# A two-layer hybrid decoder trunk: S5 block loads in a pool of their own, SSD's VectorE operations regrouped, the S5 scan on chunks between the MLA merges

## The chip, the cores and the metric

The kernel runs on one core of a Trainium2 chip. The metric is the device time of one execution in microseconds (us). Three executions of the kernel before took 1957.41 to 1961.91 us, median 1959.04.

## The reference

Each of the two layers normalises the 512 x 1024 input, multiplies it by one wide projection, and feeds three parallel causal branches: SSD (a chunked Mamba-2 scan), S5 (a diagonal complex recurrence) and MLA (latent attention). The branches are gated, summed, projected and added to the input.

```python
for l in range(2):
    h = rms_norm(x, pre_norm[l])
    z_a, xbc, dt_raw, u_b, z_b, c_q, c_kv, k_rope, z_c, gate_logits = split_columns(h @ w_in[l])
    y_a = ssd_branch(z_a, xbc, dt_raw, ...) @ w_a[l]
    y_b = s5_branch(u_b, z_b, ...) @ w_b[l]
    y_c = mla_branch(c_q, c_kv, k_rope, z_c, ...) @ w_c[l]
    g = sigmoid(gate_logits)
    x = x + rms_norm((g[0] * y_a + g[1] * y_b + g[2] * y_c) @ w_o[l], post_norm[l])
```

In SSD each head needs, for each chunk of 128 positions, exp(cs[t] - cs[s]) on and under the diagonal, multiplied with the product of C and B; x is scaled by dt, and by dt and the decay to the chunk's end for the chunk's state. In S5 the state of 64 blocks of 8 positions follows s[c+1] += a * s[c] with complex a.

## The kernel before, in words

Every float32 matrix product is made of three matmuls: each operand is split into a rounded part (`wh`, `hh`, `ah`, made by a ScalarE copy) and the rest (`wl`, `hl`, `al`, a VectorE subtraction). `split` (L83) does this for activations and `weight` (L92) for weights: a 512 KB load into a tile `wf`, the copy to `wh`, the subtraction to `wl`, each with two buffers. With `lo_pool` at n, GpSimd makes every n-th `wl` in place of VectorE, counted by `self.nw`. `dense` (L108) runs 24 matmuls of 512 columns on one weight: 16 on `wh`, then 8 on `wl`.

A layer goes through these stages: MLA, with the S5 preparation `s5_prep` filled in between; the S5 scan (`s5_scan`, L896) and the eight merges of MLA (`merge`, L470, on `w_c`, each with a gate tile); `ssd_dt` (L665), small operations for dt and its running sum; `ssd` (L723), four groups of four heads, in which the projections, the convolutions (`conv`, L739: one ScalarE and four VectorE operations on 512 columns), the heads (`head`, L848) and the states are dealt out in turn; the S5 stage (L1052), eight blocks of `silu2`, `s5_block` (L912), a merge on `w_a` and `s5_gelu`; then GLU, the merges on `w_b` and the output projection. In layer 0 the scan starts at 398 us, SSD fills about 450 to 683 us, the S5 stage 683 to 810 us; layer 1 comes some 967 us later.

All loads and stores go through SP's one queue, in order. Program order isn't the order of execution: the kernel is built under `TileContext(nc, schedule_with_timeline_sim=True)`, which lays out each engine's instructions in advance by a timeline of its own, with program order as the priority among those that are ready. Once laid out, every engine runs its instructions in that order and waits at each for what it needs.

The steps that matter here:
- The scan loads all states into `ms` (128 x 2 x 32 x 64, 2 MB), runs 63 steps of four VectorE operations on 64 elements each (L905 to L908), and stores to `sdr`. A step reads `ms[:, :, :, c]`: neighbouring elements lie 64 floats apart. In program order the scan comes ahead of the merges.
- `s5_block` loads for each block of eight groups `uf`, `sf` (from `sdr`), eight pieces of `kpad` and one of `odr`, 11 transfers and 1.5 MB, in the pool `s5`, which opens after the pool `ssd` has closed, and whose tiles take the same memory.
- `head` broadcasts one head's running sum by a matmul into `pr` (PSUM), subtracts the position's own sum and clamps at zero in four VectorE operations of 128 columns (L856), takes exp on ScalarE in one operation, multiplies and splits.
- `xe`, the state's input, is made by GpSimd from the product `xd` (L787).
- The SSD result `y` is multiplied by the norm's gain on VectorE (L844) and then split.

Of the kernel before, what the change touches and what calls it, by code (L numbers as in the profile page):

```python
# [9 lines left out]
F32 = mybir.dt.float32  # L10
F32R = mybir.dt.float32r
I32 = mybir.dt.int32
AF = mybir.ActivationFunctionType
ALU = mybir.AluOpType
# [6 lines left out]
P = 128  # L21
# [13 lines left out]
class Trunk:  # L35
# [629 lines left out]
    def ssd_dt(self, l, sp):  # L665

        nc, a, sm = self.nc, self.a, self.sm
        raw = sp.tile([P, 512], F32, name="dtraw")
# [46 lines left out]
        dte, dec = sp.tile([P, 64], F32, name="dte"), sp.tile([P, 64], F32, name="dec")  # L715
        self.tt(dte, ps[:, 0:64], cs, ALU.subtract)
        self.act_(dte, dte, AF.Exp)
        self.act_(dec, ps[:, 0:64], AF.Exp)
        self.tap(f"dt{l}", dt)
        self.tap(f"cs{l}", cs)  # L720
        return dt, cs, cs2, dte, dec

    def ssd(self, l):  # L723
        nc, tc, a = self.nc, self.tc, self.a
        with tc.tile_pool(name=f"ssd{l}", bufs=1, reuse_waits="tile") as sp:
            dt, cs, cs2, dte, dec = self.dts
            cw, cb = self.mgp.tile([P, 16, 4], F32, name="cw"), self.mgp.tile([P, 16], F32, name="cb")
            nc.sync.dma_start(cw, a["conv_w"][l])
            nc.sync.dma_start(cb, a["conv_b"][l])
# [27 lines left out]
            def core(g, xs, zs, bt, ct):  # L757
# [15 lines left out]
                for i in range(2):  # L773
                    ps = self.bank()
                    for c in range(4):
                        nc.tensor.transpose(ps[:, c * P:c * P + P], xs[i][:, c * P:c * P + P], self.ident)
                    xd = self.tmp().rearrange("p (c h d) -> p c h d", c=4, h=2)
                    hs = slice(4 * g + 2 * i, 4 * g + 2 * i + 2)
                    self.tt(
                        xd, ps.rearrange("p (c h d) -> p c h d", c=4, h=2),  # L780
                        cst(dt, 0, 4, hs).unsqueeze(3).broadcast_to([P, 4, 2, 64]), ALU.mult,
                    )
                    cc = slice(128 * i, 128 * i + 128)
                    xf = xd.rearrange("p c h d -> p c (h d)")
                    self.split(xf, xdh[:, :, cc], xdl[:, :, cc])
                    xe = sp.tile([P, 3, 2, 64], F32, name="xef", tag="xef")
                    self.gt(xe, xd[:, 0:3], cst(dte, 0, 3, hs).unsqueeze(3).broadcast_to([P, 3, 2, 64]), ALU.mult)  # L787
                    self.split(xe.rearrange("p c h d -> p c (h d)"), xeh[:, :, cc], xel[:, :, cc])
                    yield
                ps = self.bank()  # L790
# [20 lines left out]
                for i in range(2):  # L811
# [29 lines left out]
                    if pt:  # L841
                        self.gt(sq, sq, s2, ALU.add)
                    hi, lo = self.act_tile()
                    self.ts(y, y, sn[:, pt:pt + 1], None, ALU.mult)  # L844
                    self.split(y, hi, lo)
                    self.yacts.append((hi, lo))

            def head(g, hh, cbm):  # L848

                hd = 4 * g + hh  # L850
                pr = self.pq.tile([P, 512], F32, name="pr", tag=("pM", "pb")[hh % 2])
                nc.tensor.matmul(pr, self.sel[:, hd:hd + 1].broadcast_to([64, P]), cs2, start=True, stop=True)
                m = self.tmp()
                for c in range(4):
                    k = slice(c * P, c * P + P)
                    self.ts(m[:, k], pr[:, k], cs[:, 16 * c + hd:16 * c + hd + 1], 0.0, ALU.subtract, ALU.min)  # L856
                self.act_(m, m, AF.Exp)
                self.tt(m, m, cbm.rearrange("p c k -> p (c k)"), ALU.mult)
                mh, ml = r2("mm", [P, 512], 2)
                self.split(m, mh, ml)  # L860
                return mh, ml, pr
# [34 lines left out]
    def s5_scan(self, l, sp):  # L896

        nc = self.nc
        kpad, odr, msd, u2, sc1, sc2 = self.s5m[l]
        ms = sp.tile([P, 2, 32, 64], F32, name="ms")  # L900
        nc.sync.dma_start(ms, msd.rearrange("h p r g c -> (h p) r g c"))
        t1, t2 = sp.tile([P, 2, 32], F32, name="sc_t1"), sp.tile([P, 2, 32], F32, name="sc_t2")
        for c in range(63):
            s, d = ms[:, :, :, c], ms[:, :, :, c + 1]
            nc.vector.tensor_tensor(t1, sc1, s, ALU.mult)  # L905
            nc.vector.tensor_tensor(t2, sc2, s[:, ::-1], ALU.mult)
            nc.vector.tensor_tensor(d, d, t1, ALU.add)
            nc.vector.tensor_tensor(d, d, t2, ALU.add)  # L908
        self.sdr = self.dr.tile([2, 64, 2, 32, 64], F32, name=f"sdr{l}")
        nc.sync.dma_start(self.sdr.rearrange("h p r g c -> (h p) r g c"), ms)  # L910

    def s5_block(self, l, sp, b):  # L912

        nc, a = self.nc, self.a
        kpad, odr, msd, u2, sc1, sc2 = self.s5m[l]
        g8 = slice(8 * b, 8 * b + 8)

        def load(src, nm):
            f = sp.tile([P, 8, 64], F32, name=nm + "f", tag=nm + "f")
            nc.sync.dma_start(f, src)  # L920
            h, lo = (sp.tile([P, 8, 64], F32R, name=nm + x, tag=nm + x) for x in "hl")
            self.split(f, h, lo)
            return h, lo

        uh, ul = load(u2[b].rearrange("p (g c) -> p g c", g=8), "u")
        sh, sl = load(self.sdr[b // 4, :, :, 8 * (b % 4):8 * (b % 4) + 8].rearrange("p r g c -> r p g c"), "s")
        th, tl = self.weight([(slice(16 * j, 16 * j + 16), kpad[:, g8, 16 * j:16 * j + P]) for j in range(8)], 1024, sp)
        oh, ol = self.weight(odr[:, g8].rearrange("p g k -> p (g k)"), 1024, sp)
        ys = sp.tile([64, 8, 8, 16], F32, name="ys", tag="ys")
        pss = [self.pq.tile([P, 512], F32, name="pM", tag=tag) for tag in ("pM", "pb")]  # L930
        for hf in range(2):
# [78 lines left out]
    def mix(self, l):  # L1010
        nc, tc, a = self.nc, self.tc, self.a
        with ExitStack() as st:
# [27 lines left out]
                self.yacts.append((hi, lo))  # L1040
            acts, self.yacts = self.yacts, []
            with tc.tile_pool(name=f"scan{l}", bufs=1, reuse_waits="tile", side="right") as sp:
                self.s5_scan(l, sp)
                for m in range(8):
                    self.merge(l, 2, a["w_c"], acts, m)
            with tc.tile_pool(name=f"dt{l}", bufs=1, reuse_waits="tile") as dp:
                self.dts = self.ssd_dt(l, dp)
                self.lo_pool = 2
                self.ssd(l)
                self.lo_pool = 0  # L1050
            acts, self.yacts = self.yacts, []
            with tc.tile_pool(name=f"s5{l}", bufs=1, reuse_waits="tile") as sp:  # L1052
                G, gl = self.G, []
                for b in range(8):
                    if b < 6:
                        G.append(self.silu2(l, ZB + b + 2))
                    ys = self.s5_block(l, sp, b)
                    self.merge(l, 0, a["w_a"], acts, b, self.rrow)
                    gl.append(self.s5_gelu(l, sp, b, ys, G[b]))
                self.gates_ahead(l, 1, 2)  # L1060
                self.s5_glu(l, sp, gl, G)
            acts, self.yacts = self.yacts, []
            wp = st.enter_context(tc.tile_pool(name=f"wo{l}", bufs=1, reuse_waits="tile", side="right"))
            G = wp.tile([P, D], F32, name="gpost")
            nc.sync.dma_start(G, a["post_norm"][l:l + 1, :].broadcast_to([P, D]))
# [175 lines left out]
```

## Time and profile before

| | us |
|---|---|
| median of three executions | 1959.04 |
| lowest, highest | 1957.41, 1961.91 |
| the profiled execution | 1960.12 |
| its span, first to last instruction | 1958.3 |
| TensorE busy (matmuls) | 1855.4, 95% |
| VectorE busy | 1430.2, 73% |
| ScalarE busy | 913.1, 47% |
| GpSimd busy | 627.0, 32% |

[...] In what follows L12 is line 12 of the kernel, PE is TensorE, DVE VectorE, ACT ScalarE, POOL GpSimd, and SPq the queue from which SP issues transfers. Instructions are named by the tile that they write and those that they read: `wl<-wf,wh`. Most lines are those of helpers (L66 all ScalarE operations, L78 all tensor_tensor on VectorE), so groups are told apart by tile. An arrow behind a row names what ended the idle time before the instruction.

### The profile page before, as it was taken

The numbers are of one execution on the slowest core, as the hardware profiler recorded it, in microseconds if no ns is written. First come the engines' busy times: TensorE is split into PE (matmuls) and PEld (weight loads), VectorE is DVE, ScalarE is ACT, GpSimd is POOL, SyncE is SP. The second block draws the span as 40 slices with busy tenths as digits, with TensorE's granted clock in tenths as the row PEclk, the third lists the DMA queues.
The fourth block names the chain that finished last, engine by engine and source line by source line (L and its number), as shares of the span: only waits on it lengthen the run. The fifth ranks groups of instructions, "written<-read, shape, count | busy, mean of one in ns | idle before, by whom it ended". The sixth has DMA issues, their size and how long they took to land.

```text
span 1958.3 us, 28033 instructions
## 1 busy us (share of the span) xinstructions
PE 1855.4 (95%) x9880; PEld 1519.3 (78%) x9880; DVE 1430.2 (73%) x2882; ACT 913.1 (47%) x1647; POOL 627.0 (32%) x679
## 2 busy tenths in 40 slices
PE   7899998998999989999997999999999999999998
PEld 5678877686787778888886878876878887788887
DVE  6877675789999857744569667666999996776443
ACT  4356555422555545543332556554235564554431
POOL 0856575201233301201118566660023331012010
PEclk9899999899999999999998999998999999999999
DMA  5343433132322266345232334342322224662541
GB/s 162 91 122 104 125 106 116 53 137 86 116 69 65 72 175 184 108 128 185 101 85 92 112 103 136 103 130 90 98 91 103 76 76 108 184 172 86 172 129 44
DMA packets 136254, 219.99 MB, mean 112 GB/s; under 512 B 39857, under 2 KB 79409, under 8 KB 135601
## 3 DMA queue, kind: packets, MB, share of 16 engines
q1 hardware_dynamic: 136112, 218.19, 37.1%
q8 instruction: 78, 1.28, 0.3%
q14 instruction: 64, 0.52, 0.1%
HBM read 182.08 MB, written 31.33 MB: 109 GB/s over the span
## 4 chain that ended last, share of the span: by engine, by line
PE 63%; DVE 21%; DMA 8%; ACT 3%; POOL 3%; issue 2%; SPq 1%; DVEq 0%; ACTq 0%; POOLq 0%
PE mm L116 15%; PE mm L117 14%; PE mm L119 14%; DVE wl L78 3%; DVE keep L69 3%; PE mm L62 2%; PE mm L61 2%; PE mm L63 2%; DVE ms L908 2%; DMA msd<-pmo 2%; DVE sc_t L905 2%; PE aux L61 2%; PE aux L62 1%; PE aux L63 1%; PE aux L648 1%
## 5 line engine op out<-in xcount | busy, mean ns | idle before, releaser
L116 PE MATMUL mm<-hh,wh 128*128 128x512 f32 (+1 forms) x1232 | 501.0, 407 | 16.2 <-ACT wh L66 9.4
L66 ACT ACTIVATE wh<-wf 128x1024 fp32r<-128x1024 f32 (+1 forms) x294 | 291.1, 995 | 447.1 <-PE mm L117 192.7
L117 PE MATMUL mm<-hl,wh 128*128 128x512 f32 (+1 forms) x1232 | 493.1, 400 | 0.0
L78 DVE TENSOR_TENSOR wl<-wf,wh 128x1024 fp32r<-128x1024 f32 (+1 forms) x243 | 298.6, 1234 | 166.5 <-ACT wh L66 129.2
L119 PE MATMUL mm<-hh,wl 128*128 128x512 f32 (+1 forms) x1232 | 317.2, 394 | 1.4 <-DVE wl L78 1.4
L116 PEld LDWEIGHTS mm<-hh,wh 128*128 128x128 f32 (+1 forms) x1232 | 237.0, 192 | 75.2 <-issue 12.7
L117 PEld LDWEIGHTS mm<-hl,wh 128*128 128x128 f32 (+1 forms) x1232 | 236.8, 192 | 48.9 <-issue 0.7
L119 PEld LDWEIGHTS mm<-hh,wl 128*128 128x128 f32 (+1 forms) x1232 | 227.3, 187 | 51.3 <-DVE wl L78 2.5
L81 POOL TENSOR_TENSOR mg<-mg,tmp 128x512 f32<-128x512 f32 x32 | 77.7, 2432 | 456.7 <-DVE tmp L78 240.8
L81 POOL TENSOR_TENSOR wl<-wf,wh 128x1024 fp32r<-128x1024 f32 (+1 forms) x51 | 110.6, 2168 | 299.2 <-ACT wh L66 254.4
L116 PE MATMUL mm<-ah,wh 128*128 128x512 f32 x512 | 200.4, 394 | 0.0
L117 PE MATMUL mm<-al,wh 128*128 128x512 f32 x512 | 199.6, 390 | 0.0
L119 PE MATMUL mm<-ah,wl 128*128 128x512 f32 x512 | 127.6, 390 | 0.0
L116 PEld LDWEIGHTS mm<-ah,wh 128*128 128x128 f32 x512 | 96.3, 188 | 21.8 <-ACT ah L66 1.2
L117 PEld LDWEIGHTS mm<-al,wh 128*128 128x128 f32 x512 | 96.2, 188 | 20.6 <-issue 1.0
L119 PEld LDWEIGHTS mm<-ah,wl 128*128 128x128 f32 x512 | 95.7, 188 | 19.5
L626 DVE CUSTOM_DVE_ANT_0 sc<-aux,cmask 128x128 f32<-128x128 f32 (+3 forms) x128 | 61.4, 483 | 57.2 <-PE aux L63 56.4
L66 ACT ACTIVATE sc<-sc,nm 128x128 f32<-128x128 f32 (+3 forms) x128 | 70.3, 553 | 12.6 <-DVE nm L73 12.4
L66 ACT ACTIVATE tmp<-mm 128x512 f32<-128x512 f32 x76 | 44.9, 594 | 59.8 <-PE mm L63 31.5
L69 DVE SCALAR_TENSOR_TENSOR keep<-mm,cw,keep 128x511 f32<-128x511 f32 (+2 forms) x96 | 71.1, 740 | 1.4 <-ACT keep L66 1.1
L78 DVE TENSOR_TENSOR pl<-aux,ph 128x512 fp32r<-128x512 f32 (+1 forms) x96 | 55.7, 594 | 16.6 <-ACT ph L66 15.9
L66 ACT ACTIVATE tmp<-keep 128x512 f32<-128x512 f32 x48 | 30.3, 631 | 75.0 <-DVE keep L69 69.8
(346 smaller groups left out, 4001.7 us busy)
## 6 DMA issues: line engine op xcount, KB each, us to landing
wf<-in_w_in SPq DMA_DIRECT2D x156, 512.0 KB
odr<-pv SPq DMA_DIRECT2D x64, 128.0 KB
wf<-in_w_c SPq DMA_DIRECT2D x16, 512.0 KB
wf<-in_w_a SPq DMA_DIRECT2D x16, 512.0 KB
wf<-kpad SPq DMA_DIRECT2D x128, 64.0 KB
wf<-odr SPq DMA_DIRECT2D x16, 512.0 KB
wf<-in_w_glu SPq DMA_DIRECT2D x16, 512.0 KB
wf<-in_w_b SPq DMA_DIRECT2D x16, 512.0 KB
```

What stands on the lines that cost most here:

```text
L61: mm(out, ah, bh, start=start, stop=False)
L62: mm(out, ah, bl, start=False, stop=False)
L63: mm(out, al, bh, start=False, stop=stop)
L66: self.nc.scalar.activation(out, in_, func, **kw)
L69: self.nc.vector.scalar_tensor_tensor(out, in0, s, in1, op0, op1)
L78: self.nc.vector.tensor_tensor(out, a, b, op)
L81: self.nc.gpsimd.tensor_tensor(out, a, b, op)
L116: mm(ps[:m], wh[:, o(i)], bh, start=i == 0, stop=False)
L117: mm(ps[:m], wh[:, o(i)], bl, start=False, stop=False)
L119: mm(ps[:m], wl[:, o(i)], bh, start=False, stop=i == k - 1)
L626: nc.vector.tensor_tensor_reduce(out=sc, in0=ps[:, :n], in1=self.cmask[:, 512 - n:512], op0=ALU.add, op1=ALU.max, scale=1.0, scalar=-3.0e3 ...
L905: nc.vector.tensor_tensor(t1, sc1, s, ALU.mult)
```

## The change

- The scan works on chunks of eight steps. ScalarE copies a chunk into a `tmp` tile in which the 64 elements of a step lie side by side, VectorE runs the same four operations on it, ScalarE copies it back (16 copies of 512 columns per layer). The scan is now a generator: merge 0, chunk 0, merge 1, chunk 1 and so on, and its load comes after merge 0.
- The S5 loads move out of `s5_block` into `s5_load`, with a pool `s5l` that stays open from the end of the scan to the end of the S5 stage. Block 0 is loaded ahead of `ssd_dt`, block b + 1 right after block b's computation and ahead of the merge. The weights' halves no longer go through `weight`, so they don't count in `self.nw`.
- `head` takes the minimum with the position's sum in one VectorE operation of 512 columns; the subtraction becomes the bias of four ScalarE exps of 128 columns. `ssd_dt` makes the negated sum.
- `xe` is made by VectorE from PSUM, with dt multiplied into `dte` in `ssd_dt`.
- The gain moves into ScalarE's copy (scale) and VectorE's subtraction (now a scalar_tensor_tensor).

```diff
@@ ssd_dt
+        self.tt(dte, dte, dt, ALU.mult)
+        ncs = sp.tile([P, 64], F32, name="ncs")
+        self.ts(ncs, cs, -1.0, None, ALU.mult)
@@ ssd
-                    self.gt(xe, xd[:, 0:3], cst(dte, 0, 3, hs).unsqueeze(3).broadcast_to([P, 3, 2, 64]), ALU.mult)
+                    self.tt(
+                        xe, ps[:, 0:384].rearrange("p (c h d) -> p c h d", c=3, h=2),
+                        cst(dte, 0, 3, hs).unsqueeze(3).broadcast_to([P, 3, 2, 64]), ALU.mult,
+                    )
...
-                    self.ts(y, y, sn[:, pt:pt + 1], None, ALU.mult)
-                    self.split(y, hi, lo)
+                    self.act_(hi, y, AF.Identity, scale=sn[:, pt:pt + 1])
+                    self.stt(lo, y, sn[:, pt:pt + 1], hi.bitcast(F32), ALU.mult, ALU.subtract)
@@ head
+                self.tt(
+                    m.rearrange("p (c k) -> p c k", c=4), pr.rearrange("p (c k) -> p c k", c=4),
+                    cst(cs, 0, 4, hd).unsqueeze(2).broadcast_to([P, 4, P]), ALU.min,
+                )
                 for c in range(4):
                     k = slice(c * P, c * P + P)
-                    self.ts(m[:, k], pr[:, k], cs[:, 16 * c + hd:16 * c + hd + 1], 0.0, ALU.subtract, ALU.min)
-                self.act_(m, m, AF.Exp)
+                    self.act_(m[:, k], m[:, k], AF.Exp, bias=ncs[:, 16 * c + hd:16 * c + hd + 1])
@@ s5_scan
-        for c in range(63):
-            s, d = ms[:, :, :, c], ms[:, :, :, c + 1]
+        prev = None
+        for q in range(8):
+            x = self.tmp().rearrange("p (c r g) -> p c r g", c=8, r=2)
+            cq = ms[:, :, :, 8 * q:8 * q + 8].rearrange("p r g c -> p c r g")
+            self.act_(x, cq)
+            for c in range(8):
+                if q or c:
+                    s, d = (x[:, c - 1] if c else prev), x[:, c]
...
+            prev = x[:, 7]
+            if q:
+                self.act_(cq, x)
+            else:
+                self.act_(cq[:, 1:], x[:, 1:])
+            yield
@@ s5_load (new)
+        th, oh = (lp.tile([P, 1024], F32, name="wf", tag="wf", bufs=2) for _ in range(2))
+        uf, sf = (lp.tile([P, 8, 64], F32, name=nm, tag=nm) for nm in ("uf", "sf"))
+        for j in range(8):
+            rows = slice(16 * j, 16 * j + 16)
+            nc.sync.dma_start(th[rows].rearrange("p (g k) -> p g k", k=P), kpad[:, g8, 16 * j:16 * j + P])
+        nc.sync.dma_start(oh, odr[:, g8].rearrange("p g k -> p (g k)"))
+        nc.sync.dma_start(uf, u2[b].rearrange("p (g c) -> p g c", g=8))
+        nc.sync.dma_start(sf, self.sdr[b // 4, :, :, 8 * (b % 4):8 * (b % 4) + 8].rearrange("p r g c -> r p g c"))
+        return th, oh, uf, sf
@@ mix
-                self.s5_scan(l, sp)
+                scan = self.s5_scan(l, sp)
                 for m in range(8):
                     self.merge(l, 2, a["w_c"], acts, m)
+                    next(scan)
+                next(scan, None)
+            ls = st.enter_context(ExitStack())
+            lp = ls.enter_context(tc.tile_pool(name=f"s5l{l}", bufs=1, reuse_waits="tile", side="right"))
+            raw = self.s5_load(l, lp, 0)
...
-                    ys = self.s5_block(l, sp, b)
+                    ys = self.s5_block(l, sp, raw)
+                    if b < 7:
+                        raw = self.s5_load(l, lp, b + 1)
                     self.merge(l, 0, a["w_a"], acts, b, self.rrow)
...
+            ls.close()
```

## Rows read from the trace of the kernel before

**Rows 1.** windows, layer 0: busy PE, PEld, DVE, ACT, POOL; PEclk, DMA share, GB/s
```profile
395.00:440.00 45.00, 44.03 (x195) 36.17 (x194) 40.55 (x163) 11.84 (x13) 0.00 (x0) 1.00 0.36 127
440.00:510.00 70.00, 62.57 (x279) 49.03 (x277) 67.98 (x178) 22.07 (x32) 13.93 (x7) 0.98 0.32 107
510.00:690.00 180.00, 175.01 (x961) 141.61 (x961) 165.75 (x270) 97.29 (x160) 55.51 (x39) 0.99 0.24 72
690.00:740.00 50.00, 43.88 (x304) 35.20 (x303) 30.77 (x37) 25.92 (x37) 5.18 (x3) 0.97 0.66 181
```

**Rows 2.** windows, layer 1, the same stages and columns
```profile
1405.00:1455.00 50.00, 45.28 (x200) 35.72 (x199) 48.38 (x143) 13.74 (x19) 7.26 (x3) 0.97 0.28 90
1455.00:1655.00 200.00, 199.92 (x1096) 163.83 (x1096) 182.25 (x312) 111.10 (x180) 59.81 (x42) 1.00 0.29 89
1655.00:1700.00 45.00, 38.73 (x299) 31.63 (x298) 29.85 (x36) 22.60 (x32) 5.70 (x3) 0.96 0.63 175
```

**Rows 3.** waits of TensorE, 440 to 510 us: us in total, times, longest
```profile
PE mm L116 <- DVE keep L69: 4.4, 2, 3.0
```

**Rows 4.** timeline of TensorE, start of the S5 stage: start, us, what, [idle]
```profile
704.42 0.50 PE L116 MATMUL mm<-hh,wh 128*128 128x512 f32 x1 [3.40 <-ACT wh L66]
...
1662.97 0.49 PE L116 MATMUL mm<-hh,wh 128*128 128x512 f32 x1 [3.98 <-ACT wh L66]
```

**Rows 5.** timeline of the DMA queue SPq, start of S5 stage, layer 0
```profile
683.27 0.56 SPq L920 DMA_DIRECT2D sf<-sdr  x1
683.88 7.47 SPq L100 DMA_DIRECT2D wf<-kpad  x8
...
693.00 0.94 SPq L102 DMA_DIRECT2D wf<-in_w_in  x2
```

**Rows 6.** chain of waits, start of the S5 stage in layer 0
```profile
693.51 11.09 DMA wf<-in_w_in
```

**Rows 7.** groups by form on VectorE, 390 to 650 us: busy us, mean ns
```profile
L908 DVE TENSOR_TENSOR ms<-ms,sc_t 128x64 f32<-128x64 f32 x63 | 21.1, 335 | 1.4
...
L906 DVE TENSOR_TENSOR sc_t<-sc,ms 128x64 f32<-128x64 f32 x63 | 16.8, 266 | 0.0
...
L78 DVE TENSOR_TENSOR d_w<-d_w,e_out 128x64 f32<-128x64 f32 x1 | 0.2, 225 | 0.0
```

**Rows 8.** groups by form on VectorE, 510 to 690 us
```profile
L75 DVE TENSOR_SCALAR tmp<-pr,cs 128x128 f32<-128x128 f32 x64 | 17.3, 336 | 0.0
...
L78 DVE TENSOR_TENSOR xdl<-tmp,xdh 128x512 fp32r<-128x512 f32 x6 | 10.2, 1727 | 0.8 <-ACT xdh L66 0.7
L73 DVE TENSOR_SCALAR tmp<-tmp,sn 128x512 f32<-128x512 f32 x8 | 9.8, 1220 | 0.9 <-ACT tmp L66 0.7
...
L78 DVE TENSOR_TENSOR er<-aux,er 128x384 f32<-128x384 f32 x8 | 4.4, 550 | 0.0
L78 DVE TENSOR_TENSOR tmp<-aux,dt 128x512 f32<-128x512 f32 x6 | 3.8, 680 | 0.0
```

**Rows 9.** groups by form on GpSimd, 390 to 690 us
```profile
L81 POOL TENSOR_TENSOR wl<-wf,wh 128x1024 fp32r<-128x1024 f32 x14 | 36.5, 2606 | 126.0 <-ACT wh L66 107.0 <-PE mm L119 19.0
...
L81 POOL TENSOR_TENSOR xef<-tmp,dte 128x384 f32<-128x384 f32 x8 | 6.7, 836 | 28.4 <-DVE tmp L78 15.1 <-ACT tmp L66 8.0 <-DVE xel L78 5.3
```

**Rows 10.** groups by form on ScalarE: MLA, 510 to 690 us, GLU
```profile
L66 ACT ACTIVATE sc<-sc,nm 128x128 f32<-128x128 f32 x16 | 6.4, 401 | 4.5 <-DVE nm L73 4.5
...
L66 ACT ACTIVATE tmp<-tmp 128x512 f32<-128x512 f32 x23 | 14.4, 628 | 19.2 <-DVE tmp L69 12.2 <-DVE tmp L75 6.8
...
L66 ACT ACTIVATE keep<-mm,cb,cw 128x512 f32<-128x512 f32 x10 | 7.7, 766 | 0.0
...
L66 ACT ACTIVATE ah<-gl 128x512 fp32r<-128x512 f32 x6 | 6.7, 1268 | 0.0
```

**Rows 11.** timeline of VectorE: the scan's first and its last (63rd) step
```profile
398.27 0.28 DVE L905 TENSOR_TENSOR sc_t<-sc,ms 128x64 f32<-128x64 f32 x1 [8.28 <-DMA ms<-msd]
...
499.49 0.27 DVE L905 TENSOR_TENSOR sc_t<-sc,ms 128x64 f32<-128x64 f32 x1
```

More of the change, by code (lines that the diff above doesn't have):

```diff
@@ L720, in ssd_dt @@
         self.tap(f"cs{l}", cs)
-        return dt, cs, cs2, dte, dec
+        return dt, cs, ncs, cs2, dte, dec
     def ssd(self, l):
@@ L725, in ssd @@
         with tc.tile_pool(name=f"ssd{l}", bufs=1, reuse_waits="tile") as sp:
-            dt, cs, cs2, dte, dec = self.dts
+            dt, cs, ncs, cs2, dte, dec = self.dts
             cw, cb = self.mgp.tile([P, 16, 4], F32, name="cw"), self.mgp.tile([P, 16], F32, name="cb")
@@ L902, in s5_scan @@
         t1, t2 = sp.tile([P, 2, 32], F32, name="sc_t1"), sp.tile([P, 2, 32], F32, name="sc_t2")
-        for c in range(63):
-            s, d = ms[:, :, :, c], ms[:, :, :, c + 1]
[L905 to L908, printed above, removed]
+        prev = None
[6 more added lines that the diff above has]
+                    s, d = (x[:, c - 1] if c else prev), x[:, c]
+                    nc.vector.tensor_tensor(t1, sc1, s, ALU.mult)
+                    nc.vector.tensor_tensor(t2, sc2, s[:, ::-1], ALU.mult)
+                    nc.vector.tensor_tensor(d, d, t1, ALU.add)
+                    nc.vector.tensor_tensor(d, d, t2, ALU.add)
+            prev = x[:, 7]
[4 more added lines that the diff above has]
+            yield
@@ L909, in s5_scan, with s5_load @@
         self.sdr = self.dr.tile([2, 64, 2, 32, 64], F32, name=f"sdr{l}")
         nc.sync.dma_start(self.sdr.rearrange("h p r g c -> (h p) r g c"), ms)
-    def s5_block(self, l, sp, b):
-        nc, a = self.nc, self.a
+    def s5_load(self, l, lp, b):
+        nc = self.nc
         kpad, odr, msd, u2, sc1, sc2 = self.s5m[l]
         g8 = slice(8 * b, 8 * b + 8)
-        def load(src, nm):
-            f = sp.tile([P, 8, 64], F32, name=nm + "f", tag=nm + "f")
-            nc.sync.dma_start(f, src)
+        th, oh = (lp.tile([P, 1024], F32, name="wf", tag="wf", bufs=2) for _ in range(2))
[7 more added lines that the diff above has]
+        return th, oh, uf, sf
@@ L921, in load, with s5_block @@
+    def s5_block(self, l, sp, raw):
+        nc = self.nc
+        def load(f, nm):
             h, lo = (sp.tile([P, 8, 64], F32R, name=nm + x, tag=nm + x) for x in "hl")
@@ L923, in load, with halves @@
             return h, lo
[L925 to L928, printed above, removed]
+        def halves(f):
+            wh, wl = (sp.tile([P, 1024], F32R, name=x, tag=x, bufs=2) for x in ("wh", "wl"))
+            self.split(f, wh, wl)
+            return wh, wl
+        uh, ul = load(raw[2], "u")
+        sh, sl = load(raw[3], "s")
+        th, tl = halves(raw[0])
+        oh, ol = halves(raw[1])
         ys = sp.tile([64, 8, 8, 16], F32, name="ys", tag="ys")
```

## The prediction

> **What bounds the kernel now.** The page comes first: TensorE is busy 1855.4 of 1958.3 us (table above), so the change can only give back what TensorE loses in the stages that it touches. The windows view, cut at those stages, says how much that is. In layer 0 TensorE is idle 0.97 us of the merges' first 45 us, 7.43 of the 70 us in which SSD begins, 4.99 of the 180 us of SSD proper and 6.12 of the S5 stage's first 50 us [rows 1]. In layer 1 the last three are 4.72, 0.08 and 6.27 [rows 2]. That is 30.6 us in all. The granted clock adds to it: a mean of 0.98, 0.99 and 0.97 over 70, 180 and 50 us, and of 0.97 and 0.96 over 50 and 45 us, is work short by 1.4 + 1.8 + 1.5 and 1.5 + 1.8 = 8.0 us. [...]
>
> Two causes share these losses. In SSD, VectorE is busy 67.98 of 70 and 165.75 of 180 us [rows 1], and the view of waits names it: 4.4 us of the first stretch are spent on a convolution's result, `keep` [rows 3]. At the start of the S5 stage VectorE is no bound (30.77 of 50 us); there TensorE stands 3.40 us in layer 0 and 3.98 in layer 1 for one weight's `wh` [rows 4]. The queue shows why: the S5 loads can start only when SSD's tiles are free, at 683.27, the eight `kpad` pieces take SP 7.47 us, and the next projection's weight goes out at 693.00, behind two blocks' loads [rows 5]. It takes 11.09 us on the chain of waits [rows 6].
>
> **The change, part by part.**
>
> *Scan.* An operation on strided elements takes 335 to 266 ns, one on 64 that lie side by side 225 [rows 7]. With the middle, 300, a layer saves 63 x 4 x 75 ns = 18.9 us of VectorE. Added are 16 ScalarE copies.
>
> *Heads.* Four clamped subtractions keep VectorE busy 17.3 / 64 = 0.27 us each, 1.08 together; one of 512 columns from PSUM with a broadcast operand takes 0.68 [rows 8]. Sixteen heads: -6.4 us.
>
> *Gain.* Eight operations of 1.22 us go [rows 8]: -9.8 us. The subtraction becomes another of the same length: nothing.
>
> *xe.* VectorE gains eight operations of 384 columns from PSUM at 0.55 us [rows 8], +4.4. But `xdl` now takes 1.727 us against 0.68 for operations of that size [rows 8], while GpSimd makes `xef` in 0.836 [rows 9]. With `xef` gone from GpSimd that excess goes, 8 x 1.05 = 8.4, or passes to another operation that meets GpSimd; so between +4.4 and -4.0. I take -4.0, since `xef` is what GpSimd starts at that moment. [...]
>
> *dt.* Two operations of 64 elements: +0.4. Together VectorE sheds 18.9 + 6.4 + 9.8 + 4.0 - 0.4 = 38.7 us per layer, of 274.3 busy in the first three windows of layer 0 [rows 1]: 14%.
>
> What that is worth to TensorE is bounded by the losses of the SSD windows: idle 7.43 + 4.99 + 4.72 + 0.08 = 17.2, clock 1.4 + 1.8 + 1.5 = 4.7, so 0 to 21.9 us. Not all hangs on VectorE's load: a convolution is still a chain of ScalarE and VectorE operations before TensorE can go on. I take 60%: **-13.1**.
>
> *S5 loads.* Block 0's 11 transfers move from 683 us to the end of the scan, past all of SSD's weights on SP. At 683 only block 1's remain, and they wait for block 0's splits. The weight that TensorE stood for then has one block's loads ahead of it or none. I take the whole of 3.40 + 3.98 and of that clock, 1.5 + 1.8: **-10.7** (ends 0 and -10.7). The other idle time of these windows, 2.7 + 2.3 us, lies in front of later blocks, whose loads now stand ahead of a merge's weight: half, **-2.5** (ends 0 and -5.0).
>
> *Scan's load.* It no longer stands ahead of the first merge's weights: **-1.0** (ends 0 and -1.0).
>
> *New work on ScalarE.* The nearest rows give 0.401 us for an exp of 128 columns, 0.628 for one of 512, 0.766 with scale and bias from tiles, 1.268 for a copy with strided elements [rows 10]. A head adds 4 x 0.401 - 0.628 = 0.98, a layer 15.6; the scan's copies 16 x 0.628 to 16 x 1.268, I take 20.3 since they stride too; the gain 8 x 0.14 = 1.1. So +37 us per layer on an engine that is busy 131.2 of 295 us in the first three windows [rows 1]; it stays at 57%, and this work is hidden. [...]
>
> *Holds.* In order as the queues are, ScalarE's copies back wait for VectorE with weight splits queued behind them, and SP's block 0 loads wait for the store of the scan with weights behind them. The scan's load, of the same 2 MB, kept VectorE waiting 8.28 us [rows 11]; two weight buffers cover one `dense`, 24 x 44.03 / 195 = 5.4 us [rows 1], so that hold costs 0 to 2.9 us per layer. ScalarE's is the rival below. I take **+2**. Dropping 16 weights per layer from `self.nw` shifts which third of layer 1's MLA weights GpSimd splits: nothing, within one split of 2.6 us [rows 9] either way.
>
> Sum: -13.1 - 10.7 - 2.5 - 1.0 + 2 = -25.3. The profiled execution took 1960.12 us (span 1958.3 and 1.8 around it), 1.08 above the median; 1934.8 for such a one, **1934** for the median.
>
> **The rivals.**
>
> *Only the loads pay.* VectorE's relief is taken up by the chain through ScalarE, which is longer now, or by the plan that lays the order out anew. For it: layer 1 runs 200 us of SSD with VectorE at 91% and TensorE idle 0.08 [rows 2], so a full VectorE need not cost anything. Against: VectorE is the engine named in the waits [rows 3]. Then -10.7 - 2.5 - 1.0 + 2 = -12.2: 1947.
>
> *Slower: the scan holds ScalarE.* Each chunk ends in a copy that waits for its eighth step; the next merges' `wh` stand behind it. Steps go 1.63 us apart now, (499.49 - 398.27) / 62 [rows 11], a chunk takes 13.1 us; a merge with its gate is 48 matmuls, 10.8 us. If the plan puts the copy ahead of a weight that TensorE needs and the lag passes the 5.4 us of buffered work, the merges run at the scan's pace: 16 x 2.3 = 37 us, less the 14.2 of loads: 1982. Against: steps get shorter, and the merges left VectorE 4.5 us in 45 free even with the scan on top [rows 1].
>
> *It doesn't do what it says.* Block 1's loads burst at 683 in place of block 0's and the same weight is late, and in SSD the stalls only move: 1957 to 1959.
>
> **How the numbers follow.** Forecast 0.60, only the loads 0.20, no change 0.12, slower 0.08. About 0.2%, 3.9 us, is what a measurement here can tell from no change; the first two cases lie beyond it. So faster 0.80, within 0.12, slower 0.08. The low end: all ends at their best, -21.9 - 10.7 - 5.0 - 1.0 = -38.6, is 1920, and 5 us more for waits too short to show as idle, since a matmul still counts as busy while it drains: 1915. The high end takes in the second case and most of the fourth: 1957.
>
> **What would show it.** Right: in SSD VectorE falls to about 80% busy and TensorE's waits for `keep` shrink; at the start of the S5 stage no wait of 3 us for `wh`, and granted clock 1.00; scan operations near 225 ns; `xdl` near 0.69. Wrong: TensorE waits for `wh` during the merges, with ScalarE waiting for the scan's `tmp` before it; SP waiting on the store of `sdr` with weights behind it; or idle time in SSD that keeps its size under another name.

## The result, and the profile after

The changed kernel takes a median of 1952.89 us over 20 executions, the kernel before, run beside it on the same chips, 1963.28 us over 20 (1957.41 to 1967.89). The ratio is 0.9945, with a 95% interval of 0.9934 to 0.9956: faster by about 10.8 us. The forecast was 25 us; the sign and the range held, the size did not. The profiled execution took 1956.32 us (span 1954.5). That is only 3.8 us under the profiled execution of the kernel before, while the medians lie 10.4 us apart: the two traces show where time went, not the size of the whole gain.

The page says at once that the engines did what was meant and that it bought little. VectorE's busy time fell from 1430.2 to 1388.2 us, ScalarE's rose from 913.1 to 960.0, and TensorE is still busy 95% of the span:

```profile
PE 1859.5 (95%) x9880; PEld 1526.3 (78%) x9880; DVE 1388.2 (71%) x2790; ACT 960.0 (49%) x1775; POOL 625.0 (32%) x663
```

The windows view by stage, layer 0, answers to [rows 1] (the stages are now a little shorter, so the cuts differ; same columns):

```profile
395.00:440.00 45.00, 41.62 (x172) 33.87 (x171) 35.37 (x151) 19.66 (x22) 0.00 (x0) 0.92 0.33 111
440.00:510.00 70.00, 70.00 (x327) 56.90 (x326) 67.17 (x187) 37.48 (x58) 12.24 (x5) 1.00 0.36 117
510.00:672.00 162.00, 158.60 (x888) 130.15 (x887) 142.33 (x200) 96.47 (x188) 50.34 (x32) 0.98 0.25 80
672.00:725.00 53.00, 49.16 (x333) 40.45 (x333) 36.90 (x47) 27.22 (x40) 7.08 (x4) 1.00 0.64 169
```

Layer 1, to set against [rows 2]:

```profile
1400.00:1450.00 50.00, 50.00 (x237) 41.01 (x236) 46.97 (x145) 24.14 (x32) 7.69 (x3) 1.00 0.29 89
1450.00:1500.00 50.00, 42.43 (x220) 34.05 (x219) 39.19 (x57) 26.82 (x53) 10.49 (x6) 0.93 0.44 141
1500.00:1655.00 155.00, 152.37 (x850) 123.97 (x849) 130.04 (x187) 90.05 (x172) 41.31 (x28) 0.98 0.24 72
1655.00:1700.00 45.00, 42.63 (x308) 35.72 (x306) 30.12 (x35) 20.94 (x30) 6.07 (x3) 1.00 0.65 187
```

Read them as gains and losses. Gained: the stretches in which SSD begins hold no idle time (before, 7.43 us in layer 0 and 4.72 in layer 1), and the S5 stage's start keeps the full clock (0.97 and 0.96 before) with 3.84 and 2.37 us idle for 6.12 and 6.27. Lost: 3.38 us idle and a mean clock of 0.92 in layer 0's first merges, where the idle time was 0.97 at full clock; and in layer 1's SSD, which had lost 0.08 us before, 7.57 us idle at a mean clock of 0.93 in 50 us and 2.63 at 0.98 in the 155 us behind them. Over all these windows TensorE's idle time fell from 30.6 to 23.2 us, but the work that the mean clocks are short by, reckoned as in the prediction, rose from 8.0 to 13.4 us. In windows of a few microseconds that clock, a share of full speed, was, before, 0.50 from 705.1 to 708.4 us, behind the wait of 3.40 us [rows 4], and 1.00 from 709 to 740; with the change 0.50 from 401.5 to 407, behind the 3.38 us, and 0.51 from 1479 to 1483.5, at the end of the 7.57. The loss of 7.57 us is one wait. The timelines show it on TensorE, and on ScalarE just ahead of it:

```profile
1481.47 0.34 PE L61 MATMUL aux<-mmh,xdh 128*64 128x128 f32 x1 [7.57 <-DVE stf L78]
```

```profile
1478.67 1.06 ACT L66 ACTIVATE wh<-wf 128x1024 fp32r<-128x1024 f32 x1 [7.91 <-DMA wf<-in_w_in]
```

TensorE waits for a state on VectorE, VectorE for a weight's subtraction behind ScalarE, and ScalarE 7.91 us for a weight of SSD. Why that weight is late is read on the DMA queue:

```profile
1454.42 0.33 SPq L933 DMA_DIRECT2D sdr<-ms  x1
1454.84 0.38 SPq L102 DMA_DIRECT2D wf<-in_w_in  x1
1461.65 5.01 SPq L944 DMA_DIRECT2D wf<-kpad  x8
1466.70 0.43 SPq L945 DMA_DIRECT2D wf<-odr  x1
1467.18 0.43 SPq L946 DMA_DIRECT2D uf<-u  x1
1467.71 0.56 SPq L947 DMA_DIRECT2D sf<-sdr  x1
1468.37 27.91 SPq L102 DMA_DIRECT2D wf<-in_w_in  x5
```

and in the waits of that queue, 1440 to 1500 us:

```profile
SPq L933 <- ACT ms L66: 6.7, 1, 6.7
SPq L944 <- DMA sdr<-ms: 6.4, 1, 6.4
```

SP stands 6.7 us for the last ScalarE copy of the scan before it can store `sdr`, issues one weight, stands 6.4 us until the store has landed (the first piece of `kpad` waits for it, though it doesn't read `sdr`: the pool `s5l` opens when the scan's pool has closed, on the same side of the memory, so I take the wait to be for the memory of `ms`), spends 6.7 us on issuing block 0's 11 transfers, and only then issues the next weight: 13.5 us after the one before it. That weight then takes long to land, in the chain of waits:

```profile
1468.37 10.22 DMA wf<-in_w_in
```

In layer 0 the same sequence has ScalarE stand 6.15 us for the weight behind the loads and TensorE 2.87 us. So a transfer that was moved out of S5's way was put in SSD's way. Whether this is what the forecast missed is what the runs had to show.

### The profile page after: what moved, and what is told of

Its sections match the earlier page's. It is cut to its first block, busy times and chain, and to the rows that moved or that the text cites. A ratio compares the mean times of both kernels' runs of the same rounds, so it can differ in the third digit from the quotient of the medians.

```text
span 1954.5 us, 28096 instructions
## 1 busy us (share of the span) xinstructions
PE 1859.5 (95%) x9880; PEld 1526.3 (78%) x9880; DVE 1388.2 (71%) x2790; ACT 960.0 (49%) x1775; POOL 625.0 (32%) x663
## 4 chain that ended last, share of the span: by engine, by line
PE 68%; DVE 13%; DMA 9%; ACT 4%; POOL 3%; issue 2%; SPq 1%; DVEq 0%; ACTq 0%; POOLq 0%
PE mm L116 17%; PE mm L117 16%; PE mm L119 16%; DMA wf<-in_w_in 3%; DVE wl L78 3%; PE mm L61 2%; PE mm L62 2%; PE mm L63 2%; DVE keep L69 2%; PE aux L61 2%; PE aux L62 2%; PE aux L63 2%; DMA sf<-sdr 2%; PE aux L648 1%; DMA msd<-pmo 1%
## 5 line engine op out<-in xcount | busy, mean ns | idle before, releaser
L78 DVE TENSOR_TENSOR wl<-wf,wh 128x1024 fp32r<-128x1024 f32 (+1 forms) x243 | 290.8, 1203 | 161.7 <-ACT wh L66 119.2
L81 POOL TENSOR_TENSOR wl<-wf,wh 128x1024 fp32r<-128x1024 f32 (+1 forms) x51 | 115.2, 2258 | 406.4 <-PE mm L119 278.4
L66 ACT ACTIVATE sc<-sc,nm 128x128 f32<-128x128 f32 (+3 forms) x128 | 70.3, 553 | 10.3 <-DVE nm L73 10.3
L66 ACT ACTIVATE ph<-aux 128x512 fp32r<-128x512 f32 (+1 forms) x96 | 48.6, 524 | 35.0 <-PE aux L648 34.4
## 6 DMA issues: line engine op xcount, KB each, us to landing
odr<-pv SPq DMA_DIRECT2D x64, 128.0 KB
```

The source lines that it names most:

```text
L66: self.nc.scalar.activation(out, in_, func, **kw)
L78: self.nc.vector.tensor_tensor(out, a, b, op)
L81: self.nc.gpsimd.tensor_tensor(out, a, b, op)
```

## The experiments

All were timed in five rounds beside the kernel before; each ratio is to that.

**The three parts alone.** The scan alone, the SSD operations alone, the S5 loads alone, each taken from the change's own lines:

```diff
@@ SSD alone: ssd_dt, ssd and head as in the change; scan and loads as before
+                    cst(cs, 0, 4, hd).unsqueeze(2).broadcast_to([P, 4, P]), ALU.min,
...
+                    self.act_(m[:, k], m[:, k], AF.Exp, bias=ncs[:, 16 * c + hd:16 * c + hd + 1])
@@ scan alone: s5_scan and its place in mix as in the change
+                scan = self.s5_scan(l, sp)
...
+                    next(scan)
...
@@ loads alone: s5_load, s5_block and the pool as in the change
+            raw = self.s5_load(l, lp, 0)
```

> The SSD part alone (fewer VectorE operations; scan and S5 loads as before). Theory H (the relief of VectorE pays, the early S5 loads take part of it back by holding SP's queue at the start of SSD): 6 to 14 us faster than the kernel before, ratio 0.993 to 0.997; the 3 to 4 us wait for wh at the start of each S5 stage stays. Rival L (only the loads pay): no difference, ratio 0.999 to 1.001. Rival N (the longer MLA stage of layer 1 is a shift of GpSimd's turns): MLA of layer 1 as long as before, since the count of weights is unchanged; H says the same.

> The scan on chunks alone. H: the scan's operations shrink to some 225 ns, but ScalarE's copies stand in front of weight splits; together between 5 us faster and 3 us slower, ratio 0.997 to 1.0015, and in layer 0 a wait of TensorE of about 3 us for wh near 400 us. Rival A (ScalarE's copies are what cost the gain, in both layers): 4 to 12 us slower, ratio 1.002 to 1.006.

> The S5 loads ahead alone. H: the start of each S5 stage gains 2 to 4 us and its clock, the burst of the scan's store and 11 loads at the start of SSD costs 3 to 8 us per layer: between 3 us faster and 8 us slower, ratio 0.9985 to 1.004, with a wait of TensorE of several us some 20 us behind the store of sdr in at least one layer. Rival L: 8 to 14 us faster, ratio 0.993 to 0.996.

SSD alone: 0.9982 (0.9964 to 1.0000), some 3.5 us, with an interval that reaches no difference. Scan alone: 0.9933 (0.9914 to 0.9951), 13.1 us. Loads alone: 0.9968 (0.9953 to 0.9983), 6.3 us. The three add up to 22.9 us, close to the forecast, give or take some 6 by their intervals; together they give 10.8. About 12 us are lost where they meet. None of the three came out as expected: SSD alone and the loads alone lie between their two theories, the first without the wait for `wh` and the second without the wait behind the store that were foreseen, and the scan alone gained more than either of its theories allowed.

The SSD operations did not take away the waits at SSD's start, which the forecast had booked for VectorE's relief as a whole. With SSD alone, TensorE's waits from 440 to 510 us are as in [rows 3]:

```profile
PE mm L116 <- DVE keep L69: 4.5, 2, 3.1
```

The stall for `wh` at S5's start is gone in that run, but 2.0 us of new waits stand at the end of layer 1's SSD, from 1640 to 1680 us, and that layer's SSD takes 5.2 us longer than before (the table below):

```profile
PE mm L116 <- ACT ah L66: 1.1, 1, 1.1
PE aux L231 <- POOL ssq L81: 0.9, 1, 0.9
```

With the scan alone, SSD untouched, no wait for `keep` is left in either layer. Those waits came from VectorE's backlog out of the scan, not from SSD's own operations.

**Block 0's load later in program order.** The changed kernel, but block 0's `s5_load` is called at the start of the S5 stage:

```diff
-            raw = self.s5_load(l, lp, 0)
...
                 G, gl = self.G, []
+                raw = self.s5_load(l, lp, 0)
```

> The whole change, but block 0's 11 loads come in program order at the start of the S5 stage in place of ahead of ssd_dt. H: the stall of 7.6 us at the start of layer 1's SSD goes with its half clock, the wait of 3 to 4 us for wh at the start of the S5 stages comes back: 2 to 8 us faster than the changed kernel, ratio to before 0.990 to 0.9935. Rival A (the copies hold ScalarE, the loads cost nothing where they were): 4 to 8 us slower than the changed kernel, ratio 0.997 to 0.999.

0.9895 (0.9873 to 0.9917), 1944.34 us: half a per cent better than the changed kernel, a little more than the 2 to 8 us expected and not in the expected way: the load was to go back to S5, with the wait for `wh` there. The load had not gone back. It waits for nothing but its memory, and the plan lets it go as soon as it can; program order only gave it a lower rank. The queue in layer 1:

```profile
1446.25 0.33 SPq L933 DMA_DIRECT2D sdr<-ms  x1
1446.67 0.38 SPq L102 DMA_DIRECT2D wf<-in_w_in  x1
1453.48 0.34 SPq L944 DMA_DIRECT2D wf<-kpad  x1
1453.92 0.37 SPq L102 DMA_DIRECT2D wf<-in_w_in  x1
1454.34 4.32 SPq L944 DMA_DIRECT2D wf<-kpad  x7
...
1461.73 29.03 SPq L102 DMA_DIRECT2D wf<-in_w_in  x5
```

The first piece of `kpad` is issued 7.2 us after the store, as in the changed kernel; but now one weight goes between the pieces, so that weights go out 7.25 and 7.8 us apart and not 13.5. TensorE is busy 47.44 of the 50 us from 1450 us on (42.43 with the change) at a clock of 1.00. So the load can go out at the same hour and cost little, if weights of SSD go between its pieces.

**On that base: the GpSimd count, SSD, the scan, more buffers.** Four runs with the late load, each with one thing put back or added:

```diff
@@ count: halves in s5_block
+            self.nw += 1
@@ no SSD: ssd_dt, ssd and head as before
@@ no scan: s5_scan and its place in mix as before
@@ two buffers: s5_load
-        uf, sf = (lp.tile([P, 8, 64], F32, name=nm, tag=nm) for nm in ("uf", "sf"))
+        uf, sf = (lp.tile([P, 8, 64], F32, name=nm, tag=nm, bufs=2) for nm in ("uf", "sf"))
```

> The kernel with block 0's loads ranked behind SSD's weights (e4), and the S5 halves counted in self.nw again. Rival N (the shift of GpSimd's turns lengthened layer 1's MLA from 339.6 to 344 us): MLA of layer 1 back near 340 us, 3 to 5 us faster than e4, ratio to before 0.987 to 0.988. H (MLA differs as much between executions): within 1.5 us of e4, ratio 0.9885 to 0.991.

> e4 without the SSD regrouping: scan on chunks and S5 loads, block 0 ranked behind the weights. H2 (the waits at SSD's start were the scan's, and the regrouping of SSD only moves idle time to SSD's end): within 4 us of e4, ratio to before 0.988 to 0.992. H (the regrouping takes part of the 13 us that the prediction gave it): 6 to 13 us slower than e4, ratio 0.9925 to 0.996.

> e4 with the old scan: SSD regrouping and S5 loads. H2: the waits for keep and cfl at the start of SSD come back (7 us in layer 0, 4 in layer 1, with their clock): 8 to 14 us slower than e4, ratio to before 0.9935 to 0.997. H: 3 to 7 us slower, ratio 0.991 to 0.993.

> e4 with two buffers for uf and sf, so that they are loaded a block further ahead. H: the wait for sh at the start of the S5 stage (2.6 us in layer 0, 1.25 in layer 1) goes: 2 to 5 us faster than e4, ratio to before 0.987 to 0.9885. Rival (the wait is set by the queue, not by the buffer): no difference from e4, 0.9885 to 0.9905.

Count: 0.9907 (0.9891 to 0.9923), no different from 0.9895; the shift of `self.nw` is worth nothing, as forecast. No SSD: 0.9895 (0.9879 to 0.9911), the same to the last digit: on top of scan and loads the SSD operations pay nothing. By the profiled executions that is a sum of two shifts: with them scan and SSD take 10.0 us less in layer 0 (277.4 for 287.4) and 9.1 more in layer 1 (284.8 for 275.7). No scan: 0.9979 (0.9962 to 0.9997), so the scan is worth 16 us here, a little more than expected, and the waits for `keep` return. Two buffers: 0.9921 (0.9905 to 0.9937), where 2 to 5 us of gain were expected: 5 us worse by the ratios, though the intervals overlap. Now the second block's `uf` and `sf` wait for nothing either and go out with the first ahead of a weight:

```profile
1466.82 0.46 SPq L946 DMA_DIRECT2D uf<-u  x1
1467.32 1.02 SPq L947 DMA_DIRECT2D sf<-sdr  x1
1468.44 18.75 SPq L102 DMA_DIRECT2D wf<-in_w_in  x3
```

and TensorE waits again, from 1475 to 1495 us:

```profile
PE mm L116 <- ACT wh L66: 3.0, 1, 3.0
PE aux L61 <- ACT mmh L66: 1.6, 1, 1.6
```

**The scan taken apart.** Its two halves on the kernel before: the old strided steps dealt out between the merges, and the compact chunks all ahead of them.

```diff
@@ spread alone: s5_scan
-        for c in range(63):
+        for q in range(8):
+            for c in range(max(8 * q - 1, 0), 8 * q + 7):
...
+            yield
@@ chunks alone: mix (s5_scan as in the change)
-                self.s5_scan(l, sp)
+                for _ in self.s5_scan(l, sp):
+                    pass
```

> The kernel before with the scan's 63 steps (still on the strided layout, no ScalarE copies) issued in eight portions between the merges. Theory S (the scan's gain comes from where its steps stand: merges' evictions are no longer behind the scan on VectorE, and the scan's end falls at the merges' end): 0.992 to 0.995 of the kernel before, about 1951 us, as the whole scan change alone (0.9933), and the waits for keep and cfl at SSD's start go. Rival L (the gain comes from the shorter operations on the compact layout): 0.998 to 1.001, the waits for keep and cfl stay at 4 to 10 us per layer.

> The kernel before with the scan on compact chunks (copied in and out by ScalarE), all of it still issued ahead of the merges. Theory S (place of the steps): 0.998 to 1.001 of the kernel before, waits at SSD's start stay. Rival L (shorter operations: VectorE's scan steps take some 19 us less per layer, so that its backlog is gone before SSD): 0.992 to 0.995, waits for keep and cfl at SSD's start gone. In both the 11 ScalarE copies ahead of the merges' weights can cost up to 3 us at the first merge.

Neither theory holds by itself, and the second run is slower than both allowed. Spread alone: 1.0001 (0.9990 to 1.0012), with the waits for `keep` unchanged:

```profile
PE mm L116 <- DVE keep L69: 4.4, 2, 3.0
```

Chunks alone: 1.0127 (1.0108 to 1.0145), slower by 25 us. SSD's start is clear of its waits, but ScalarE stands 10.48 us for the load of `ms`, then makes seven chunks' copies in 6.95 us, all ahead of the merges' weights, and TensorE stops, from 395 to 432 us:

```profile
PE aux L701 <- DVE adt L69: 10.2, 1, 10.2
PE mm L116 <- ACT tmp L66: 5.6, 1, 5.6
```

The second wait, 5.6 us, is the prediction's slower rival at work: the merge's copy on ScalarE stands behind a chunk's copy back, which had waited 4.50 us for VectorE's steps. The clock falls too: 0.78 and 0.67 in the two windows of the waits, 1.00 right after.

```profile
395.00:420.00 25.00, 14.17 (x66) 10.97 (x66) 15.01 (x72) 10.26 (x12) 0.00 (x0) 0.78 0.48 171
420.00:440.00 20.00, 13.57 (x46) 10.37 (x47) 16.95 (x85) 6.92 (x12) 0.00 (x0) 0.67 0.07 21
440.00:460.00 20.00, 20.00 (x90) 16.55 (x89) 16.85 (x68) 7.34 (x8) 0.00 (x0) 1.00 0.27 85
```

In this run TensorE's 17.3 us of standing gave VectorE time as well, so that it alone doesn't show what cleared SSD's start; but steps that were spread and not shortened left the waits, and with both they are gone at a wait of 3.4 us. The gain needs both.

**The load truly held back.** Four one-column VectorE copies into block 0's tiles, after SSD's second group, keep its transfers off the queue until then; once on the changed kernel, once with two buffers and SSD as before, once with two buffers and the change's SSD.

```diff
@@ ssd, after the second group (g == 1)
+                    self.raw0 = self.s5_load(l, self.lp0, 0, sq[:, 0:1])
...
@@ s5_load
+            for t in (th[:, 0:1], oh[:, 0:1], uf[:, 0, 0:1], sf[:, 0, 0:1]):
+                nc.vector.tensor_copy(t, after)
```

> The changed kernel with the loads of S5's block 0 held back, by four one-column VectorE copies into their tiles, until SSD's second group is over. Theory Q (block 0's loads and the hold for the scan's store stand ahead of SSD's weights on SP's queue): the 7.6 us stall of layer 1's SSD start is gone as in the run with the late load, 0.986 to 0.990 of the kernel before, about 1940 us. Rival M (the place of the loads costs nothing; the run with the late load was faster for some other reason, such as the order the planner then finds): about 0.9945, as the changed kernel.

> The kernel before with the changed scan and the S5 loads in their own pool, held back until SSD's second group is over, with two buffers for uf and sf so that the second block is not held either; SSD as before the change. If SSD's regrouping is worth nothing on top of the scan (as with the late load) and the loads stand clear of SSD's start: 0.985 to 0.989, about 1937 us, with no stall over 2 us at SSD's start or at S5's start. If the regrouping is needed once the loads no longer bound the stage: 0.990 to 0.994, with VectorE late at SSD's end.

> The held-back loads with two buffers for uf and sf, this time with SSD's regrouping. If the regrouping pays once neither SSD's start nor S5's start is bound by loads (the 5.5 us stall for stf on VectorE at 613 us in layer 0 shrinks): 0.984 to 0.986, some 4 us under the same kernel without it (0.988). If VectorE's load in SSD bounds nothing any more: 0.987 to 0.990, and the idle time that is left stands before weights and at SSD's end.

Held back: 0.9897 (0.9879 to 0.9915), as with the late rank; the 7.57 us wait is gone. Two buffers without the SSD operations: 0.9880 (0.9859 to 0.9901), 1940.27 us; with them 0.9882 (0.9867 to 0.9897), 1938.84. So the second buffer costs nothing once the loads are held back, and the SSD operations again change nothing. The first of the two still has, where the expectation allowed 2 us, a wait of 5.46 us for VectorE's `stf` in layer 0, the second one of 4.73 in the same place: in both, ScalarE and VectorE behind it had stood about 5 us for a weight issued after the held-back loads. These two have the lowest ratios of the study, 0.6% under the changed kernel.

**The change without its loads.** Scan and SSD as in the change, `s5_block` as before:

```diff
-            raw = self.s5_load(l, lp, 0)
...
-                    ys = self.s5_block(l, sp, raw)
+                    ys = self.s5_block(l, sp, b)
```

> The changed kernel without the S5 loads in their own pool. Theory Q (block 0's loads ahead of SSD's weights cost about 10 us and pay about 6 at S5's start): 0.990 to 0.993 of the kernel before, so faster than the whole change (0.9945), with no stall over 3 us at either SSD start and S5's start stalls of 3 to 4 us in both layers back. Rival (the loads are worth in the whole change what they are worth alone, 6 us): 0.997 to 0.999.

0.9906 (0.9889 to 0.9922), 1943.59 us. Taking the loads out makes the changed kernel faster by 0.39% of 1963, 7.7 us (some 4 either way by the intervals). The store stands as long for ScalarE's copy as with the change, 6.7 us, but no load follows it, and the weights keep their pace:

```profile
1454.47 0.33 SPq L933 DMA_DIRECT2D sdr<-ms  x1
1454.88 0.38 SPq L102 DMA_DIRECT2D wf<-in_w_in  x1
...
1461.45 0.33 SPq L102 DMA_DIRECT2D wf<-in_w_in  x1
...
1466.77 0.33 SPq L102 DMA_DIRECT2D wf<-in_w_in  x1
```

TensorE's row for the 50 us that lost 7.57 with the change:

```profile
1450.00:1500.00 50.00, 49.70 (x269) 39.77 (x267) 44.69 (x62) 29.67 (x57) 15.45 (x9) 1.00 0.35 119
```

One part of the expectation missed: the S5 stalls of 3 to 4 us did not return under their old name. The longest single wait at S5's start is 1.8 us, and layer 1 shows the two waits at SSD's end that the SSD operations alone had shown.

How long the stages take shows where the loads cost and where they pay. Scan and SSD are counted here from the issue of the load of `ms` to the first matmul of `aux<-ones,ssq` (L231) behind SSD, the S5 stage from there to the first issue of a load of `w_b`; each figure is from one profiled execution, in us.

| | before | SSD alone | scan alone | loads alone | without the loads | changed |
|---|---|---|---|---|---|---|
| layer 0, scan and SSD | 291.7 | 288.9 | 285.5 | 292.3 | 277.4 | 283.6 |
| layer 0, S5 | 175.8 | 176.1 | 176.4 | 170.5 | 176.0 | 171.9 |
| layer 1, scan and SSD | 283.7 | 288.9 | 276.2 | 286.8 | 282.1 | 290.4 |
| layer 1, S5 | 176.0 | 172.6 | 175.6 | 171.9 | 172.1 | 172.7 |

On top of scan and SSD the loads make scan and SSD 6.2 and 8.3 us longer, and the S5 stages together 3.5 us shorter, nearly all of it in layer 0: layer 1's S5 stage is as short without them. Alone they cost 0.6 and 3.1 us in front and pay 5.3 and 4.1 at S5.

## Why the prediction was right or wrong

**Holds, +2: the step that failed.** The prediction named the mechanism, block 0's loads waiting for the scan's store with weights behind them, and listed it among the signs of being wrong, but priced the wait alone, 0 to 2.9 us per layer. Behind the wait come two more terms on the same queue: 6.7 us to issue the 11 transfers, and a landing time of 10.2 us for the weight issued right behind their 1.5 MB. Against 5.4 us of buffered work, the distance between weights was 13.5 us. In the place of +2, scan and SSD took 6.2 + 8.3 = 14.5 us longer with the loads than without, by the profiled executions. Put together, the three terms that concern the loads were forecast at -11.2 us; in place, against scan and SSD alone, they measured +7.7. Giving the loads a lower rank, or holding them back, brought the kernel to within some 2 us of the run without loads. With two buffers it came out 3 to 5 us under that run by the medians, but the intervals overlap: that the loads pay anything on top of the rest is not shown. The prediction's reading of the queue was also off in two points, which don't change its terms. The weight at 693.00 stood behind block 0's loads and only `uf` and `sf` of block 1, whose `kpad` follows at 695.48. And the 11.09 us are those of the second of the two weights issued there; ScalarE took the first, which TensorE waited for, at 703.32, 10.3 us after its issue.

**S5 start, -10.7, and later blocks, -2.5.** The stall for `wh` did go, and the loads alone paid 6.3 us. The idle time was not all of one cause, though: with the SSD operations alone the stall went too, and its time came back at SSD's end. So for the forecast of 13.2 us the two S5 stages are 3.9 and 3.3 us shorter than before, and only 3.5 us together than in the run without the loads. The two named stalls lasted 3.40 and 3.98 us, 7.4 together; 7.2 us is what the stages gave. The clock that the forecast counted with them, 1.5 + 1.8 us, did come back in these windows: a mean of 1.00 where 0.97 and 0.96 had been.

**SSD relief, -13.1: size near by luck, cause wrong.** Scan and SSD operations together gave 18.5 us (the forecast for them, with the scan's load, was 14.1). But the scan did it: 13.1 us alone, and 16 us where it was taken out, against 3.5 for the SSD operations alone and none on top. The sum treated all 38.7 us per layer of VectorE as equal; only those that stood ahead of SSD's start were seen to pay. The third rival's clause, that in SSD the stalls only move, was right for the SSD operations: alone they made layer 1's S5 stage 3.4 us shorter and its SSD 5.2 us longer.

**The VectorE terms themselves.** Over both layers VectorE lost 42.0 us of busy time, forecast 77.4. The groups over the whole span say where it fell short; the heads, from [rows 8], came as reckoned, 0.68 us for one operation:

```profile
L78 DVE TENSOR_TENSOR tmp<-pr,cs 128x512 f32<-128x512 f32 x32 | 20.5, 676 | 0.0
...
L78 DVE TENSOR_TENSOR xdl<-tmp,xdh 128x512 fp32r<-128x512 f32 x16 | 12.5, 780 | 0.6 <-ACT xdh L66 0.6
...
L78 DVE TENSOR_TENSOR mml<-tmp,mmh 128x512 fp32r<-128x512 f32 x32 | 27.4, 872 | 1.2 <-ACT mmh L66 1.2
```

The scan's four groups sum to 128.0 us for 504 operations, 0.254 each, where 147.3 us before is 0.292: the gain is 9.7 us per layer, not 18.9, because before's mean is 0.29 and the compact steps reach 0.225 in only one of the four groups (0.30, 0.22, 0.23, 0.27). The excess on `xdl` was read from six operations in one window, 1.05 us each; over all 16 the mean before is 1.24 us, an excess of 0.56. Of that 0.46 us each went, 7.4 in all, but `mml` rose from 0.69 to 0.87 us, 5.7 in all: the other end of the bound, the excess passing to another operation. By the times in the traces, `xdl` and `mml` never take more than 0.69 us where no GpSimd instruction runs at the same time. Before, seven `xdl` met one, 1.96 us on average, and four of these met not `xef` but a weight's `wl`; with the change three still meet a `wl`, and seven `mml` that meet GpSimd take 1.55, where ten that met it before took 0.72. The gain's term was short for the like reason: the new `al` operations take 1.30 us where the old ones took 1.00, and 15 of 16 now run beside a GpSimd instruction (1.34 us; the other one 0.75) where 5 of 16 did. The operations that the gain's term took away had met GpSimd as well: before, 15 of 16 `tmp<-tmp,sn` ran beside one of its instructions and took 1.22 us on average, the other one 0.48. VectorE's busy share in SSD went to 88% in layer 0 and 84% in layer 1, not to 80%.

**ScalarE's work, hidden.** Busy time rose by 46.9 us, forecast 74. In layer 0, 390 to 690 us:

```profile
L66 ACT ACTIVATE tmp<-tmp,ncs 128x128 f32<-128x128 f32 x64 | 20.0, 390 | 6.3 <-DVE tmp L78 6.3
...
L66 ACT ACTIVATE tmp<-ms 128x512 f32<-128x512 f32 x8 | 8.8, 1118 | 10.5 <-DMA ms<-msd 10.5
```

Four exps lie partly over each other, 20.0 us for 64, so a layer's heads added 20.0 - 16 x 0.63 = 9.9 us where 15.6 was reckoned. Hidden it was, but for one place: ScalarE stands 10.50 us for the load of `ms`, then three copies of 1.07 to 1.13 us go ahead of a merge's `wh`, and TensorE stands 3.38 us at 401.57, with a mean clock of 0.92 over the 45 us. The scan does hold ScalarE there, as the slower rival has it, but through its load and not through its eighth step, and in layer 0 only.

**The scan's load, -1.0, and `self.nw`, 0.** The first had no ground: in layer 0's queue the load still goes out ahead of the two weights, as at 390.56 before.

```profile
388.85 0.34 SPq L911 DMA_DIRECT2D ms<-msd  x1
389.29 0.38 SPq L102 DMA_DIRECT2D wf<-in_w_in  x1
```

The second held. **Slower, the scan holds ScalarE**, 37 us at the merges' pace, did not happen; the chunks without the spread show that it was near: 17.3 us idle in 45 us of layer 0's merges. **Only the loads pay**, a gain of 12.2 us, came nearest to the 10.8 measured and was the wrong way round: the loads were the part that didn't pay. The 5 us at the low end of the range, for waits too short to show as idle, were the author's estimate, and no run shows them. The trace of before has only that matmul records overlap: one of `mm<-ah,wh` lasts 0.39 us on average, where [rows 1] have 44.03 / 195 = 0.23 us busy for each.

Left open: the stage of MLA in layer 1 (from ScalarE's copy into `krdt` to the load of `ms`) takes 340 to 346 us over the kernels, 4.8 us longer in the changed kernel than in the profile of before. TensorE is idle 25.1 us of it before and 25.2 after and busy 4.65 us longer on as many matmuls, with a mean granted clock of 0.945 before and 0.936 after, worth 3.4 of the 4.8 us; the count for GpSimd was ruled out as its cause, and why the clock differs is not shown. Why the loads alone paid 6.3 us, while on top of scan and SSD operations they cost 7.7, is shown in part. In the run of the loads alone a weight goes out between the store and the loads, so that SP stands 3.6 us in place of 6.4 and weights are 10.2 us apart in place of 13.5; TensorE's longest wait in the rest of that SSD is 0.5 us.

```profile
1464.40 0.33 SPq L102 DMA_DIRECT2D wf<-in_w_in  x1
1468.32 4.59 SPq L921 DMA_DIRECT2D wf<-kpad  x8
...
1474.57 43.38 SPq L102 DMA_DIRECT2D wf<-in_w_in  x7
```

And layer 1's S5 stage had nothing left to give once the SSD operations were in: 172.6 us with them alone, 172.1 on top of the scan, 172.7 with the loads. Not tested: loads into memory that `ms` doesn't hold, which would end the wait for the store if it is for that memory, and loads from a second issuing engine.

## What to carry to other kernels

A transfer brought forward on a queue that issues in order cost what stood behind it: add the wait that it carries (here 6.4 us), the time to issue all its pieces (6.7) and the longer landing of the next transfer (10.2, where a weight between the pieces took 6.28), and set the sum against the buffered work of the engine behind (5.4, reckoned from [rows 1]). A lower rank, by issuing it later in program order, is one line, and holding it back with a small dependency a few more; here either was enough (0.9895 and 0.9897 against 0.9945). And before an engine's saved time is turned into a gain, take the parts one at a time: a stall that vanishes may stand further on, as 2.0 us did at SSD's end with the SSD operations alone.

## What the hardware showed

- A ScalarE copy of 512 columns that gathers with a stride (`tmp<-ms`) took 1.12 us on average with the change, a plain one 0.63 [rows 10].
- A 512 KB weight issued between two of the `kpad` pieces landed in 6.28 us, the one issued right after all 11 transfers in 10.45, on the chain of waits of the late load:

```profile
1446.25 7.21 DMA sdr<-ms
...
1453.92 6.28 DMA wf<-in_w_in
1461.73 10.45 DMA wf<-in_w_in
```

- A VectorE subtraction of 512 columns (`xdl`, `mml`) took 0.68 us, 0.69 at most, beside no GpSimd instruction; beside one `xdl` took 1.96 us on average before and 1.22 after, `mml` 0.72 before and 1.55 after.
- The granted clock did not follow the length of one wait. Before, it was 0.50 from 1442.4 to 1445.7 us, behind a wait of 2.16 us for `keep`; with the change it was 1.00 from 302.5 to 312 us, behind a wait of 2.23 us for `wl`.
